# A block of small matmuls on a constant tile, run ahead of the first norm of a hybrid RWKV-7 / attention encoder

## The chip, the cores and the metric

The kernel runs on one core of one Trainium2 chip. The time is that of the device, in microseconds (us), for one execution of the whole program. The median of three runs before the change is 4313.76 us (4312.27 to 4315.98). The core has five engines that this text names by the profile's short names: PE (TensorE, matmuls; PEld is its weight loads, which overlap with the matmuls), DVE (VectorE), ACT (ScalarE), POOL (GpSimd) and SP (SyncE, which here issues DMAs). Each works through its own instructions in order and waits on semaphores for the others.

## The reference

Two requests, 256 and 1024 tokens of 1024 channels, go through the same two layers. Layer 0 mixes tokens with a bidirectional RWKV-7 recurrence, layer 1 with neighbourhood attention, and each is followed by a squared-ReLU MLP. Everything is float32. The part around the change is the very start: the norm of layer 0, the token-shift mixes that read the normalised `h`, and the first projections.

```python
def _rms_norm(x, g):
    xf = x.astype(jnp.float32)
    y = xf * lax.rsqrt(jnp.mean(jnp.square(xf), axis=-1, keepdims=True) + RMS_EPS)
    return y.astype(x.dtype) * g

def _rwkv7_mixer(h, ...):
    zero = jnp.zeros_like(h[:, :1])
    xx = 0.5 * (jnp.concatenate([zero, h[:, :-1]], axis=1) + jnp.concatenate([h[:, 1:], zero], axis=1)) - h
    r, k, v = jnp.einsum('sbtc,scd->sbtd', h[None] + xx[None] * mix[:3, None, None, :], w_rkv)
    xw = h + xx * mix[3]
    xa = h + xx * mix[4]
    xg = h + xx * mix[5]
...
def _trunk(x, p):
    for layer in range(DEPTH):
        h = _rms_norm(x, p['norm_mix_g'][layer])
        ...
```

## The kernel before

Both requests lie side by side as 1280 token columns, channels on the partitions in eight tiles of 128 (`KT`). The columns are cut into three segments, 256, 512 and 512 (`SEGS`). A dense product is made of three matmuls on reduced-precision halves of its operands (`mm3`, lines 95 to 99): each operand is split into a high and a low part, a weight by ACT's copy (line 91) and POOL's subtraction (line 92), an activation by ACT (line 166) and DVE (line 167). Plain float32 operands are used elsewhere, in the norm among others.

`l0_proj` (from line 102) is the first stage. SP loads `h` by segments, and the first three blocks of `w_k` between them (`early`). `norm(s)` (line 140) squares the eight channel tiles of a segment on ACT (line 147, two buffers), sums them over the channels with a float32 matmul against a tile of ones (line 148), so that each output row holds the sum, takes the inverse root on DVE and ACT (lines 152 and 1192 to 1196) and scales `h` in place on DVE (line 155). `mix` (line 157) then makes one of the six mixes of one channel tile: ACT (161), POOL (163), DVE (164), and the split (166, 167). `project` runs the dense products of `w_k` (lines 97 to 99 again) with the mixes of later segments and two LoRA products (`lora_first`, mixes by `mix2`, lines 173 to 184, split 271 and 272) put between them. The norms of the three segments stand at the head of the queue `mixq` of mixes.

In this stage no order is written out by hand: a scheduler places the instructions of each engine, by the order in the program and by its own idea of when each is ready. From `prep_open` on, at about 317 us, PE, DVE, ACT and POOL follow an order that is written by hand through due times (`at`), within `tc.manual_schedule`. The recurrence, the output layer, attention and the second layer come after that.

PSUM, in which matmuls write, is given out in pools. The stage opens `pnA` (one tile) and `pdA` (four tiles `ps`, two of `lps`), each tile 128 x 512 float32. SBUF pools with `side="right"` (`hp`, `wkA`, `wpA`) lie at the other end of SBUF from the rest (`mixp`).

Rows of other lines that the text uses as prices: lines 292 (sums of squares of k, 512 columns), 607 (LoRA second products, weights on 64 partitions, the two directions on the two partition halves in turn), 903 and 921 (32 x 32 tiles), 953 and 1023 (128 x 128 float32), 1613 (two columns), 1845 and 1876 (attention's output, 64 weight columns, the two heads on the two column halves in turn).

Of the kernel before, what the change touches and what calls it, by code (L numbers as in the profile page):

```python
# [5 lines left out]
F32 = mybir.dt.float32  # L6
# [4 lines left out]
PSUM = bass.MemoryType.PSUM  # L11
DRAM = bass.MemoryType.DRAM

P = 128
# [34 lines left out]
class Trunk:  # L49
# [49 lines left out]
        mm(ps, sl, mh, start=False, stop=last)  # L99


    def l0_proj(self):
        nc, tc, a = self.nc, self.tc, self.a
        k_d = self.dram("k_d", [8, P, T])
# [7 lines left out]
        pos = [1, 258, 770]  # L112
        W = 1283

        mixctx = ExitStack()
        mixp = mixctx.enter_context(tc.tile_pool(name="mixp", bufs=1))
        hctx = ExitStack()
# [224 lines left out]
        w = [self.wsplit(wp, a["w_r"][m], 1024, nc.gpsimd, hb=3, rb=1) for m in range(2)]  # L342
# [1618 lines left out]
```

## Time and profile before

| what | value |
|---|---|
| median of three runs | 4313.76 us |
| the profiled execution | 4314.01 us |
| its span, first to last instruction | 4312.1 us |
| mean granted TensorE clock | 0.958 |
| first load of `h` issued | 1.64 us |
| first matmul of the norm | 5.95 us |
| DVE's first step of the first norm | 12.95 us |
| hand-ordered part begins | about 317 us |

Times in the views are microseconds from the first instruction. A timeline row has the start, the length, the engine, the line of the kernel, the operation, the tiles (output <- inputs), rows * columns of the weight, the shape of the moving tile, its type as the profile shows it, and a count of merged records; in brackets stands the idle time before it and what ended it. A row of one line's instructions gives the count and the shortest, the median and the longest duration in ns. A stage row has the length, and for each engine the busy time and the number of instructions. Matmuls are pipelined, so a record's length includes the time until its result has left the array; how fast records follow each other is read from their starts.

### The profile page before, as it was taken

What the parts mean: (1) busy time and instruction counts of PE and PEld (TensorE: products, weight loads), DVE (VectorE), ACT (ScalarE), POOL (GpSimd) and SP (SyncE); (2) the same over time, 40 slices, a digit from 0 to 9 for tenths busy, and PEclk for the clock granted to TensorE, in tenths of its full rate; (3) what the DMA queues carried; (4) which work ended last, traced back from release to release, by engine and by line L of the source; (5) the groups of instructions that cost most, each with busy time, mean ns of one, the idle gap of its engine ahead of it and who ended that gap; (6) DMA issues with size and microseconds to landing.
All of it is one profiled execution on the core that took longest, in us unless ns stands there. A gap on an engine that the chain in (4) does not pass through costs nothing.

```text
span 4312.1 us, 69598 instructions
## 1 busy us (share of the span) xinstructions
PE 3991.1 (93%) x25060; PEld 3342.6 (78%) x25060; DVE 2660.7 (62%) x5390; ACT 1813.1 (42%) x4803; POOL 1426.1 (33%) x1498
## 2 busy tenths in 40 slices
PE   7888878888998879999999998999998999999999
PEld 4665668777777758888888888877676888888888
DVE  7889963577787654755555555166665655555555
ACT  6766641677777753111111123355554311111111
POOL 5440001234444443422222234144444432222222
PEclk9997879899999989999999999999998999999999
DMA  3335565566666434111111104333335211111111
GB/s 120 81 107 198 196 201 144 141 157 155 153 151 153 108 97 133 38 39 36 40 35 40 40 31 152 117 72 77 78 70 161 65 40 40 40 35 39 35 40 59
DMA packets 484537, 400.25 MB, mean 93 GB/s; under 512 B 289216, under 2 KB 392864, under 8 KB 484192
## 3 DMA queue, kind: packets, MB, share of 16 engines
q1 hardware_dynamic: 447968, 328.56, 28.1%
q10 hardware_dynamic: 34416, 61.35, 3.9%
q0 software_dynamic: 1808, 5.90, 0.4%
q8 instruction: 197, 3.23, 0.3%
q14 instruction: 148, 1.21, 0.1%
HBM read 285.66 MB, written 121.24 MB: 94 GB/s over the span
## 4 chain that ended last, share of the span: by engine, by line
PE 69%; DVE 14%; ACT 6%; DMA 5%; issue 4%; POOL 2%; SPq 1%; ACTq 0%; DVEq 0%; POOLq 0%
PE ps L97 17%; PE ps L99 16%; PE ps L98 16%; PE w L1060 2%; PE us L1032 2%; PE kps L953 1%; PE aps L812 1%; PE vps L503 1%; PE vps L505 1%; PE vps L504 1%; PE op L1876 1%; PE us L1046 1%; PE w L1012 1%; DVE S L1054 1%; ACT u L1041 1%
## 5 line engine op out<-in xcount | busy, mean ns | idle before, releaser
L1433 DVE TENSOR_TENSOR x<-ps,x 128x256 f32<-128x256 f32 x1488 | 814.1, 595 | 628.3 <-PE ps L99 628.0
L97 PE MATMUL ps<-ah,whi 128*128 128x512 f32 (+1 forms) x2304 | 843.1, 366 | 5.0 <-ACT whi L91 4.2
L99 PE MATMUL ps<-ah,wlo 128*128 128x512 f32 (+1 forms) x2304 | 824.0, 358 | 2.1 <-POOL wlo L92 2.0
L98 PE MATMUL ps<-al,whi 128*128 128x512 f32 (+1 forms) x2304 | 823.5, 357 | 2.6 <-POOL al L1323 2.6
L92 POOL TENSOR_TENSOR wlo<-raw,whi 128x1024 fp32r<-128x1024 f32 (+1 forms) x178 | 390.5, 2194 | 851.9 <-ACT whi L91 807.8
L97 PE MATMUL ps<-hh,whi 128*128 128x512 f32 (+1 forms) x1536 | 546.9, 356 | 13.8 <-DVE x L1433 13.8
L99 PE MATMUL ps<-hh,wlo 128*128 128x512 f32 (+1 forms) x1536 | 545.9, 355 | 0.0
L98 PE MATMUL ps<-hl,whi 128*128 128x512 f32 (+1 forms) x1536 | 545.2, 355 | 0.0
L97 PEld LDWEIGHTS ps<-ah,whi 128*128 128x128 f32 x2304 | 438.8, 190 | 80.2 <-issue 13.1
L91 ACT CAST whi<-raw 128x1024 fp32r<-128x1024 f32 (+1 forms) x206 | 200.7, 975 | 696.5 <-PE ps L98 630.6
L99 PEld LDWEIGHTS ps<-ah,wlo 128*128 128x128 f32 x2304 | 437.8, 190 | 67.8 <-POOL wlo L92 2.9
L98 PEld LDWEIGHTS ps<-al,whi 128*128 128x128 f32 x2304 | 438.5, 190 | 63.0 <-POOL al L1323 2.9
L1412 POOL TENSOR_TENSOR rl<-rl 128x512 f32<-128x512 f32 (+1 forms) x192 | 174.3, 908 | 500.6 <-PE ps L99 458.3
L97 PEld LDWEIGHTS ps<-hh,whi 128*128 128x128 f32 x1536 | 291.4, 190 | 57.4 <-DVE x L1433 16.8
L1411 ACT ACTIVATE rl<-ps 128x512 f32<-128x512 f32 (+1 forms) x192 | 100.8, 525 | 546.4 <-PE ps L99 546.4
L98 PEld LDWEIGHTS ps<-hl,whi 128*128 128x128 f32 x1536 | 291.4, 190 | 41.0
L99 PEld LDWEIGHTS ps<-hh,wlo 128*128 128x128 f32 x1536 | 291.4, 190 | 41.1
L1414 ACT CAST hh<-rl 128x512 fp32r<-128x512 f32 (+1 forms) x192 | 105.5, 549 | 321.0 <-POOL rl L1412 320.9
L1054 DVE SCALAR_TENSOR_TENSOR S<-us,dall,sd 64x64 f32<-64x64 f32 x512 | 145.0, 283 | 126.4 <-PE us L1046 115.7
L1415 DVE TENSOR_TENSOR hl<-rl,hh 128x512 fp32r<-128x512 f32 (+1 forms) x192 | 119.4, 622 | 151.6 <-ACT hh L1414 151.1
L1016 POOL TENSOR_TENSOR sd<-S,dall 128x128 f32<-128x128 f32 x256 | 122.5, 480 | 258.2 <-DVE S L1054 174.8
L1060 PE MATMUL w<-u,zb 128*128 128x128 f32 x640 | 158.2, 330 | 47.0 <-ACT u L1041 44.8
(310 smaller groups left out, 8222.4 us busy)
## 6 DMA issues: line engine op xcount, KB each, us to landing
raw<-in_w_down_dram SPq DMA_DIRECT2D x64, 512.0 KB, 3.5
raw<-in_w_up_dram SPq DMA_DIRECT2D x64, 512.0 KB, 3.4
ar<-ar_d SPq DMA_DIRECT2D x80, 256.0 KB, 3.4
bk<-bk_d SPq DMA_DIRECT2D x80, 256.0 KB, 3.5
ar_d<-ar ACTq DMA_DIRECT2D x32, 512.0 KB, 2.7
bk_d<-bk ACTq DMA_DIRECT2D x32, 512.0 KB
bs<-tab SPq DMA_DIRECT2D x128, 96.0 KB, 3.9
v_d<-vt ACTq DMA_DIRECT2D x80, 128.0 KB, 4.0
```

The lines of the kernel that those rows point to most:

```text
L91: nc.scalar.copy(hi[:, cs], raw)
L92: lo_eng.tensor_tensor(out=lo[:, cs], in0=raw, in1=hi[:, cs].bitcast(F32), op=ALU.subtract)
L97: mm(ps, sh, mh, start=first, stop=False)
L98: mm(ps, sh, ml, start=False, stop=False)
L99: mm(ps, sl, mh, start=False, stop=last)
L1016: nc.gpsimd.tensor_tensor(out=R["sd"], in0=st["S"], in1=self.dall[:, m, d, ch:ch + 1].to_broadcast([P, P]), op=ALU.mult)
L1054: nc.vector.scalar_tensor_tensor(out=S2[es, es], in0=sn[es, es], scalar=D, in1=R["sd"][es, es], op0=ALU.mult, op1=ALU.add)
L1060: nc.tensor.matmul(w, J["zb"][d, g][:, c, :], R["u2"], start=False, stop=True, skip_group_check=True)
L1412: nc.gpsimd.tensor_tensor(out=r[:, :n], in0=r[:, :n], in1=r[:, :n], op=ALU.mult)
L1414: nc.scalar.copy(hh[:, :n], r[:, :n])
L1415: nc.vector.tensor_tensor(out=hl[:, :n], in0=r[:, :n], in1=hh[:, :n].bitcast(F32), op=ALU.subtract)
L1433: nc.vector.tensor_tensor(out=xv, in0=ps[:, :n], in1=xv, op=ALU.add)
```

## The change

A method `small_products` is added, and `l0_proj` calls it ahead of all its pools. It fills one SBUF tile with ones (DVE), opens eight PSUM tiles, and issues twelve loops of float32 matmuls, 286 in all, with that tile as both operands. PE keeps to the order written. `full` uses the whole 128 x 128 array. `quad(r, c, ...)` takes 64 partitions (row half `r`) and by default 64 weight columns that go to output partitions of column half `c`; with `64, 128` it uses a row half and all 128 columns. The last loop uses all rows and a column half. Both pools are closed before the stage opens its own. Nothing reads the eight tiles.

```diff
+    def small_products(self):
+
+        nc, tc = self.nc, self.tc
+        mm = nc.tensor.matmul
+        with tc.tile_pool(name="prw", bufs=1) as sp, tc.tile_pool(name="prp", bufs=1, space=PSUM) as pp:
+            x = sp.tile([P, 512], F32, name="prx")
+            nc.vector.memset(x, 1.0)
+            b = [pp.tile([P, 512], F32, name=f"pr{i}") for i in range(8)]
+            w = x[:, 0:P]
+
+            def quad(r, c, n, i, k=64, m=64):
+                rs = slice(k * r, k * r + k)
+                mm(b[i][m * c:m * c + m, :n], w[rs, :m], x[rs, :n], start=True, stop=True)
+
+            def full(n, i):
+                mm(b[i][:, :n], w, x[:, :n], start=True, stop=True)
+            with tc.manual_schedule(engines={mybir.EngineType.PE}):
+                for i in range(14):
+                    full(512, i % 8)
+                for i in range(24):
+                    full(128, i % 8)
+                for i in range(24):
+                    full(64, i % 8)
+                for i in range(24):
+                    quad(i % 2, i % 2, 64, i % 2)
+                for i in range(24):
+                    quad(0, i % 2, 64, i % 2 * 2)
+                for i in range(32):
+                    quad(i % 2, i // 2 % 2, 64, i % 4)
+                for i in range(24):
+                    quad(i % 2, i // 2 % 2, 128, i % 4)
+                for i in range(24):
+                    quad(i % 2, 0, 128, i % 2, 64, 128)
+                for i in range(24):
+                    quad(i % 2, 0, 64, i % 2, 64, 128)
+                for i in range(8):
+                    full(128, i % 2)
+                    quad(0, 0, 64, 2)
+                    quad(1, 1, 64, 3)
+                for i in range(8):
+                    quad(i % 2, 0, 128, 4 + i % 2, 64, 128)
+                    quad(0, 0, 64, 2)
+                    quad(1, 1, 64, 3)
+                for i in range(24):
+                    mm(b[i % 8][64 * (i % 2):64 * (i % 2) + 64, :64], w[:, :64], x[:, :64], start=True, stop=True)
...
     def l0_proj(self):
...
         pos = [1, 258, 770]
         W = 1283
 
+        self.small_products()
         mixctx = ExitStack()
```

## The prediction

> **What bounds the kernel now.** I read the page's first part, then the timeline and the chain of waits of the first 110 us, then tables by stage, and last the rows of small matmuls anywhere in the span that can price the new ones. A difference under 0.2% (8.6 us) can't be told from no change here; the three runs of before span 3.7 us.
>
> ```profile
> span 4312.1 us, 69598 instructions
> PE 3991.1 (93%) x25060; PEld 3342.6 (78%) x25060; DVE 2660.7 (62%) x5390; ACT 1813.1 (42%) x4803; POOL 1426.1 (33%) x1498
> ```
>
> Over the span TensorE (PE) is the busiest. The change sits at the very start, though, and there another engine decides. PE's timeline of that start (start, length, engine, line, tiles, shape, count):
>
> ```profile
> 5.95 4.65 PE L148 MATMUL ps<-sq,ones 128*128 128x256 f32 x10 [5.95 <-ACT sq L147]
> 11.01 6.87 PE L148 MATMUL ps<-sq,ones 128*128 128x256 f32 x16 [0.41 <-ACT sq L147]
> 19.25 1.12 PE L148 MATMUL ps<-sq,ones 128*128 128x512 f32 x2 [1.37 <-ACT sq L147]
> 28.16 5.46 PE L148 MATMUL ps<-sq,ones 128*128 128x512 f32 x8 [7.79 <-ACT sq L147]
> ```
>
> PE does nothing before 5.95 us, while the first inputs are loaded, and has long holes later. Stage by stage (length; busy PE, PEld, DVE, ACT, POOL; granted clock; DMA share; GB/s):
>
> ```profile
> 13.00:33.00 20.00, 10.78 (x19) 3.75 (x20) 16.77 (x29) 15.04 (x30) 9.70 (x11) 0.74 0.56 201
> 33.00:57.00 24.00, 16.92 (x92) 11.34 (x90) 20.44 (x25) 12.46 (x23) 10.88 (x7) 0.97 0.26 83
> 57.00:85.00 28.00, 22.23 (x74) 15.16 (x75) 28.00 (x28) 18.30 (x30) 20.43 (x15) 0.85 0.02 9
> 85.00:110.00 25.00, 24.63 (x100) 15.78 (x99) 14.24 (x22) 15.35 (x30) 12.13 (x12) 1.00 0.40 138
> 110.00:150.00 40.00, 36.92 (x232) 30.70 (x231) 35.82 (x60) 31.87 (x68) 16.21 (x19) 1.00 0.29 55
> 150.00:200.00 50.00, 42.33 (x237) 32.20 (x236) 45.30 (x74) 36.73 (x81) 25.22 (x27) 0.97 0.29 88
> 200.00:250.00 50.00, 44.75 (x273) 33.70 (x272) 47.60 (x92) 38.30 (x98) 23.55 (x31) 1.00 0.35 118
> 250.00:300.00 50.00, 44.74 (x199) 32.84 (x200) 48.30 (x64) 36.07 (x70) 29.02 (x25) 0.93 0.12 41
> ```
>
> From 13 us on VectorE (DVE) is full: 28.00 of 28.00 from 57 to 85 us, and 256.47 of the 287 us of all eight rows. What it works on hangs on the first norm, since every mix reads the normalised h. DVE's first piece of that is this row, and everything behind it starts later by as much as this row does:
>
> ```profile
> 12.95 0.42 DVE L152 TENSOR_SCALAR nx<-ps 128x256 f32<-128x256 f32 x1 [9.23 <-PE ps L148]
> ```
>
> **The change, part by part.** It adds one DVE memset and 286 float32 matmuls on PE. They write eight PSUM tiles of 128x512 float32. The norm's PSUM pools are opened after the block's pool has been closed and take its space over, so I have PE run the whole block before the norm's first matmul. Inside it PE waits for the memset alone, and nothing reads the results.
>
> *What one record costs.* L148 (below) shows 16 records of 256 columns for the eight matmuls of the first norm, and the page has as many weight loads (PEld) as matmul records: a float32 matmul is two records, each with its own weight load, though L148's weight (ones) never changes. So the constant tile saves no loads. Prices are pitches: (length of a burst − length of one) / (count − 1).
>
> ```profile
> L148 PE MATMUL ps<-sq,ones x48: 379/594/1222, 5.9 to 41.3; 128*128 128x512 f32 x32, 128*128 128x256 f32 x16
> 921.25 0.61 PE L953 MATMUL kps<-ar,bdk 128*128 128x128 f32 x4
> L953 PE MATMUL kps<-ar,bdk x640: 275/275/582, 744.9 to 1531.4; 128*128 128x128 f32 x160
> 96.10 1.03 PE L292 MATMUL nps<-ksq,cst 128*16 128x512 f32 x2
> L292 PE MATMUL nps<-ksq,cst x6: 592/597/603, 87.3 to 96.5; 128*16 128x512 f32 x6
> 2762.01 0.95 PE L1613 MATMUL nst<-cst,sq 128*128 128x2 f32 x8
> L1613 PE MATMUL nst<-cst,sq x320: 165/251/352, 2756.0 to 3238.9; 128*128 128x2 f32 x160
> ```
>
> - 128 wide, whole array: (0.61 − 0.275)/3 = 0.112 us a record, 0.223 a matmul.
> - 512 wide: 1.03 − 0.60 = 0.43 a record, 0.86 a matmul.
> - 2 wide: (0.95 − 0.25)/7 = 0.100. A record of 2 columns costs nearly what one of 128 does, so a full weight load sets a floor of about 0.10; 64 wide lies between, 0.106.
>
> ```profile
> 2874.21 0.40 PE L99 MATMUL ps<-ah,wlo 128*128 128x512 f32 x1
> 2874.54 0.45 PE L1845 MATMUL op<-s,vs 128*64 128x64 f32 x8
> 2874.92 0.50 PE L97 MATMUL ps<-ah,whi 128*128 128x512 f32 x1
> 2875.26 0.39 PE L98 MATMUL ps<-al,whi 128*128 128x512 f32 x1
> 2875.49 0.40 PE L99 MATMUL ps<-ah,wlo 128*128 128x512 f32 x1
> L1845 PE MATMUL op<-s,vs x128: 222/222/369, 2805.4 to 3273.7; 128*64 128x64 f32 x128
> 2812.45 0.88 PE L1876 MATMUL op<-s,vs 128*64 128x128 f32 x12
> L1876 PE MATMUL op<-s,vs x732: 272/273/476, 2812.4 to 3295.0; 128*64 128x128 f32 x183
> 390.04 1.02 PE L607 MATMUL l<-ta,wa 64*128 64x512 f32 x4
> 1017.08 0.40 PE L903 MATMUL yps<-qx,zb 32*32 32x32 f32 x13
> L903 PE MATMUL yps<-qx,zb x1280: 191/191/258, 752.2 to 1537.3; 32*32 32x32 f32 x183
> ```
>
> - 64 wide, two column halves in turn: (0.45 − 0.222)/7 = 0.033.
> - 128 wide in halves: with a single one at 0.273, (0.88 − 0.273)/11 = 0.055, half of the whole array's 0.112: two halves run at once.
> - Two row halves: four 512-wide records in 1.02 us, where the whole array would need 3 × 0.43 + 0.60 = 1.89: at once as well. Row and column in turn: (0.40 − 0.191)/12 = 0.017 for 32-wide tiles.
> - Going from whole to tiled and back: L1845 starts 0.33 after L99 where 0.23 is the pitch (2875.26 to 2875.49), +0.10; L97 starts 0.15 after the last tiled record (2874.54 + 0.45 − 0.22 = 2874.77) where a pair's pitch is 0.066, +0.08; the next record comes after 0.34, +0.11. About 0.30 a round trip.
>
> *The sum.* The twelve loops in their order, in us, with low and high in brackets. Low is the smallest pitch or four tiles at once; high is tiles strictly in turn, twice the paired pitch.
> 1. 14 × 512: 14 × 0.86 = 12.0, plus a slow start. The norm's first ten records of 256 columns take 4.65 us, about 0.45 each once the last one's tail is taken off, twice the 0.215 that half of 0.43 would be; the second run, from 11.01 on, has full speed in it (L148's shortest record takes 0.379). That is some 5 us at half speed, a loss of 2.5 (1.7 to 3.4). 14.5 (13.7; 15.4).
> 2. 24 × 128: 5.4 (5.4; 5.4). 3. 24 × 64: 48 × 0.106 = 5.1 (4.8; 5.4).
> 4. and 5. 24 quads each, 64 wide: 48 × 0.033 = 1.6 each (1.6; 3.1). 6. 32 quads over four tiles: 64 × 0.033 = 2.1 (1.1; 4.2).
> 7. 24 quads, 128 wide: 48 × 0.055 = 2.6 (1.3; 5.3).
> 8. and 9. 24 row halves with a 128-wide weight: 48 × 0.056 = 2.7 each (2.7; 5.4).
> 10. 8 × (whole + two quads): 0.223 + 4 × 0.033 + 0.30 = 0.65, 5.2 (2.9 with no switch cost; 6.0).
> 11. The same with a row half for the whole: 5.2 (2.8; 6.0). No row shows a row half against a quarter; I take the price of the only switch shown.
> 12. 24 column halves: 1.6 (1.6; 3.1). The other switches between loops: 0.7 (0; 1).
>
> Together 51 us (42; 69).
>
> [...]
>
> *Where it lies.* PE can begin once the memset is done. The nearest row is GpSimd's memset of a quarter of the size, and it also shows when engines are let go:
>
> ```profile
> 0.74 0.20 POOL L134 MEMSET ones<- 128x128 f32 x1 [0.29 <-POOLq L1949]
> ```
>
> 0.74 + 0.2 to 0.8 + a handoff: 1.4 (1.0; 1.8). The block ends at 1.4 + 51 = 52.4. The norm's squares wait in ScalarE's two buffers; the rest of the norm is PE and ScalarE in turn, eight steps at a warm 0.45 (two 256-wide records 0.43) and a handoff, 3.8 us, so nx starts at 56.2 instead of 12.95: **+43.2**. What hides part: before, this stretch was partly DMA time, and that is over by then; it is in the 3.8 against 7.0 (5.95 to 12.95) already.
>
> More comes back behind it. Weight casts (ScalarE) and their low parts (POOL) of three w_k blocks and the first LoRA weight don't need the norm, and can run in the block. Before, they got in DVE's way:
>
> ```profile
> 21.54 4.06 DVE L167 TENSOR_TENSOR ml<-mu,mh 128x256 fp32r<-128x256 f32 x3
> 27.06 1.50 DVE L167 TENSOR_TENSOR ml<-mu,mh 128x256 fp32r<-128x256 f32 x3
> 34.99 2.18 DVE L1194 TENSOR_TENSOR nt<-nr 128x512 f32<-128x512 f32 x1 [2.48 <-ACT nr L1193]
> 46.01 0.82 DVE L1194 TENSOR_TENSOR nt<-nr 128x512 f32<-128x512 f32 x1 [1.36 <-ACT nr L1193]
> 21.29 2.52 POOL L92 TENSOR_TENSOR wlo<-raw,whi 128x1024 fp32r<-128x1024 f32 x1
> 34.24 2.38 POOL L256 TENSOR_TENSOR lw<-lraw,lw 128x1024 fp32r<-128x1024 f32 x1
> ```
>
> Beside a POOL low part the same DVE work takes 2.6 and 1.4 longer, and the wait before L1194 is 1.1 longer: 5 us that can go. At most 10: these 4.0 and nearly all of DVE's idle from 13 to 57 us (3.2 + 3.6, less what the norm's own steps need). At least 0. I take 5: **+38**.
>
> Nothing downstream has room to take it back: the stage is full on DVE (rows above) until the hand-ordered part, which moves as a whole. The profiled execution took 4314.01 us, 1.9 around its span; 4314.0 + 38 = 4352. It lies 0.25 above the median, so the forecast for the median is the same.
>
> **The rivals.**
> *Tiles in turn.* Loops 4 to 12 gain nothing from halves, or the queue can't feed them so fast: block 69, +18 on the forecast, 4370. For it: the bursts above have 4 to 13 records, while here some 350 follow each other, and a burst may live from what was queued. Against it: every tiled row runs in pairs. [...]
> *Shorter and better covered.* Block 42 and 10 regained: 43.2 − 8.8 − 10 = +24, 4338. For it: four tiles at once need only the spacing of L903's records; ScalarE and POOL have 50 us to run ahead.
> *Not slower.* The first stage's order comes from a scheduler, not by hand, and shifts with the norm. If the new order closed DVE's holes up to the hand-ordered part, 287 − 256.5 = 30.5 us, and the POOL collisions, 4.0, it would leave 43.2 − 34.5 = +8.7, at the edge of no change: 4322. It decides only if nearly every hole closes, and they are waits in a chain of dependent steps (L1194 waits for ScalarE).
> *The block isn't there.* Nobody reads its results; dropped at compile time, it leaves a memset under the wait for DMA: 4314. Nothing in the trace shows unread work, so neither for nor against.
>
> **How the numbers follow.** Forecast 0.62 (4343 to 4361), tiles in turn 0.15, shorter 0.17, not slower 0.03, not there 0.03. The range reaches to both rivals on the slow side: 4338 to 4370; left out are the last two and the outer parts of the other rivals, under 0.2. Slower by over 0.2% 0.94, within 0.05, faster 0.01 (the not-slower case overshooting).
>
> **What would show it.** Right: about 572 new PE records ending near 52 us, nx at 56, DVE busy without holes from there, tiled loops at 0.03 to 0.06 a record, the rest of the timeline as before but later by some 38 us. Wrong: nx much before 45 or after 70; loop 11 without switch costs; wlo still beside the mixes (then +43); or a shift that shrinks between 85 and 300 us.

## The result, and the profile after

The changed kernel takes 4352.89 us in the median of three runs (4352.88 to 4353.92), against 4313.76 before: a ratio of 1.0091 with a 95% interval of 1.0068 to 1.0114. That is 39 us slower, where 38 were forecast. Its profiled execution took 4352.88 us with a span of 4351.1, so the time around the span is 1.8 us, as before. The mean granted clock is 0.959 (before 0.958).

The page's first part, after:

```profile
span 4351.1 us, 70740 instructions
PE 4038.9 (93%) x25632; PEld 3379.3 (78%) x25632; DVE 2656.5 (61%) x5391; ACT 1813.5 (42%) x4803; POOL 1426.1 (33%) x1498
```

There are 572 more matmul records, 286 times two, and as many more weight loads; one more DVE instruction is the memset. PE is busy 47.8 us longer. Nothing else has more to do. Lines of the old code stand 47 further down from here on (the norm's matmul L148 is L195).

PE's timeline of the start, after (of loop 10 only the first round and the start of the second are shown, and a row can merge several loops):

```profile
1.46 24.48 PE L117 MATMUL pr<-prx 128*128 128x512 f32 x124 [1.46 <-DVE prx L108]
25.87 10.76 PE L114 MATMUL pr<-prx 64*64 64x64 f32 x304
36.56 0.49 PE L117 MATMUL pr<-prx 128*128 128x128 f32 x2
36.98 0.33 PE L114 MATMUL pr<-prx 64*64 64x64 f32 x4
37.24 0.49 PE L117 MATMUL pr<-prx 128*128 128x128 f32 x2
...
41.74 6.98 PE L114 MATMUL pr<-prx 64*64 64x64 f32 x52
48.65 2.83 PE L146 MATMUL pr<-prx 128*64 128x64 f32 x48
51.63 5.07 PE L195 MATMUL ps<-sq,ones 128*128 128x256 f32 x16 [0.16 <-PE pr L146]
```

The block runs without a gap from 1.46 to 51.63 us, 50.2 us, and the norm's first matmul starts at its end, where it started at 5.95 before. DVE's first step of the norm, and the last `mu` of the first 24 mixes (the second row; before it was at 84.84, in the third):

```profile
56.75 0.42 DVE L199 TENSOR_SCALAR nx<-ps 128x256 f32<-128x256 f32 x1 [53.02 <-PE ps L195]
...
124.83 1.10 DVE L211 SCALAR_TENSOR_TENSOR mu<-ms,hm,mu 128x512 f32<-128x512 f32 x1
```

```profile
84.84 1.10 DVE L164 SCALAR_TENSOR_TENSOR mu<-ms,hm,mu 128x512 f32<-128x512 f32 x1
```

So `nx` is 43.8 us late, and 68 us further on DVE is 40.0 us late: 3.8 us have come back. The start of the hand-ordered part in the two kernels (before, then after):

```profile
303.94 0.17 DVE L549 TENSOR_SCALAR hw<-vec 128x32 f32<-128x32 f32 x1
```

```profile
346.35 0.17 DVE L596 TENSOR_SCALAR hw<-vec 128x32 f32<-128x32 f32 x1
```

It is 42.4 us late there, and at the end of the span 39.0. Matching DVE's instructions one by one, the delay goes up and down in between, from some 34 us (34.0 at 1531 us of before) to some 45 (44.6 at 3141 us). DVE works in the same order there as before, and PE nearly so. The first fall, from 42.4 to 37.4 within 130 us of that start, goes with a higher granted clock. Two stages of 100 us from that start on (length; busy PE, PEld, DVE, ACT, POOL; granted clock; DMA share; GB/s), first before, then after:

```profile
304.00:404.00 100.00, 81.70 (x277) 51.49 (x276) 75.33 (x141) 61.37 (x129) 0.00 (x0) 0.69 0.58 203
```

```profile
346.30:446.30 100.00, 80.20 (x286) 50.31 (x285) 79.44 (x147) 65.07 (x136) 0.00 (x0) 0.73 0.60 210
```

After, the clock is higher and PE gets nine more records done in the same 100 us.

The block itself, with the clock, by stages of the same form:

```profile
14.00:42.00 28.00, 28.00 (x451) 25.47 (x451) 0.00 (x0) 4.18 (x4) 9.43 (x5) 1.00 0.52 183
42.00:45.00 3.00, 3.00 (x30) 2.25 (x26) 0.00 (x0) 0.00 (x0) 0.00 (x0) 1.00 0.21 81
45.00:49.00 4.00, 4.00 (x30) 2.79 (x30) 0.00 (x0) 0.00 (x0) 0.00 (x0) 0.57 0.00 0
49.00:52.00 3.00, 2.84 (x49) 2.68 (x46) 0.00 (x0) 0.00 (x0) 0.00 (x0) 0.50 0.00 0
52.00:57.00 5.00, 4.49 (x17) 2.37 (x16) 0.25 (x1) 3.18 (x8) 0.00 (x0) 0.96 0.00 0
```

From 45.54 to 52.37 us the granted clock was halved, though PE had been busy without a gap for 44 us. Loop 11 runs there, and loop 12. The first row also shows what ACT and POOL did meanwhile: four casts, and as many low parts with the end of an earlier one. Their own timelines have `whi` at 10.59, 17.78 and 26.45, `wlo` at 11.71, 18.90 and 27.57, and `lw` on POOL at 29.90 and 37.61, all before the first mix.

The twelve loops, each from the start of its first record to that of the next loop's first, against the forecast:

| loop | forecast us (low; high) | measured us |
|---|---|---|
| 1: 14 x 512 | 14.5 (13.7; 15.4) | 13.66 |
| 2: 24 x 128 | 5.4 | 5.36 |
| 3: 24 x 64 | 5.1 (4.8; 5.4) | 5.40 |
| 4: quads, both halves in turn | 1.6 (1.6; 3.1) | 1.40 |
| 5: quads, column halves in turn | 1.6 (1.6; 3.1) | 1.35 |
| 6: four quads in turn, 64 wide | 2.1 (1.1; 4.2) | 0.97 |
| 7: four quads in turn, 128 wide | 2.6 (1.3; 5.3) | 1.46 |
| 8: row halves, 128 wide | 2.7 (2.7; 5.4) | 2.78 |
| 9: row halves, 64 wide | 2.7 (2.7; 5.4) | 2.72 |
| 10: whole and two quads | 5.2 (2.9; 6.0) | 5.44 |
| 11: row half and two quads | 5.2 (2.8; 6.0) | 6.65 |
| 12: column halves | 1.6 (1.6; 3.1) | 2.99 |
| switches between loops | 0.7 (0; 1) | within the above |
| all | 51 (42; 69) | 50.2 |

### The profile page after: what moved, and what is told of

Read it like the earlier page. It is cut to its first block, busy times and chain, and to the rows that moved or that the text cites. A ratio compares the mean times of both kernels' runs of the same rounds, so it can differ in the third digit from the quotient of the medians.

```text
span 4351.1 us, 70740 instructions
## 1 busy us (share of the span) xinstructions
PE 4038.9 (93%) x25632; PEld 3379.3 (78%) x25632; DVE 2656.5 (61%) x5391; ACT 1813.5 (42%) x4803; POOL 1426.1 (33%) x1498
## 4 chain that ended last, share of the span: by engine, by line
PE 70%; DVE 13%; ACT 6%; issue 3%; DMA 3%; POOL 2%; SPq 1%; ACTq 0%; DVEq 0%; POOLq 0%
PE ps L97 17%; PE ps L99 16%; PE ps L98 16%; PE w L1107 2%; PE us L1079 2%; PE kps L1000 2%; PE vps L550 1%; PE vps L552 1%; PE vps L551 1%; PE aps L859 1%; PE w L1059 1%; ACT u L1088 1%; PE us L1093 1%; ACT u L1074 1%; DVE S L1101 1%
## 5 line engine op out<-in xcount | busy, mean ns | idle before, releaser
L99 PEld LDWEIGHTS ps<-ah,wlo 128*128 128x128 f32 x2304 | 437.9, 190 | 67.8 <-POOL wlo L92 2.7
L98 PEld LDWEIGHTS ps<-hl,whi 128*128 128x128 f32 x1536 | 291.7, 190 | 41.1
```

The source lines that it names most:

```text
L98: mm(ps, sh, ml, start=False, stop=False)
```

## The experiments

Theory A throughout is the prediction's: the time grows by what `nx` is delayed, less a small fixed sum that the casts give back, and by nothing else. The rivals stand in each expectation. The runs of the kernel before that ran beside the experiments had medians of 4311.95 to 4316.16 us, each with a spread of 16 to 23 us from its fastest to its slowest, so ratios are to the runs on the same chip, and a gain or loss given as "about" is worked out from the ratio. The traces carry what the times can't tell: `nx`, and the last `mu` of the first 24 mixes, called "mix 24" below. Between them lie 71.9 us before and 68.1 after.

**The block cut short, doubled, or only its memset.** Three kernels have loops 1 to 3 alone, the whole block twice, and no matmul at all:

```diff
             with tc.manual_schedule(engines={mybir.EngineType.PE}):
                 for i in range(14):
                     full(512, i % 8)
                 for i in range(24):
                     full(128, i % 8)
                 for i in range(24):
                     full(64, i % 8)
-                for i in range(24):
-                    quad(i % 2, i % 2, 64, i % 2)
...
```

> Loops 4 to 12 are left out; the block then ends near 25.9 us. Theory A (what counts is how late the first norm ends; that is passed on whole, less some 4 us that the weight casts give back): nx at about 30.7 us, 17.8 later than in the kernel before, time +14 (+11 to +18), about 4328. Theory B (the rest of the stage takes back a fixed share: 39.1 us lost for 50.2 of block, 0.78): 0.78 x 24.4 = +19, 4333. Theory C (added PE work costs wherever it stands): +24.

Measured: 4334.6 us, ratio 1.0044 (1.0027 to 1.0061), about +19. The block ran from 1.46 to 27.50 (loop 1 took 15.07 here), and `nx` started at 32.73, +19.8. That is just beyond theory A's +11 to +18 and equal to theory B's +19; with an interval of +12 to +26 the time alone does not part them. The trace shows where theory A's sum was off: loop 1 took longer, and mix 24 came 71.3 us after `nx`, so 0.6 us came back instead of 3.8. Timelines of DVE and of POOL in this run:

```profile
35.62 6.42 DVE L180 SCALAR_TENSOR_TENSOR h<-h,vec,nr 128x256 f32<-128x256 f32 x8
```

```profile
37.68 2.53 POOL L281 TENSOR_TENSOR lw<-lraw,lw 128x1024 fp32r<-128x1024 f32 x1
```

The last low part runs at the same time as in the full block (37.61, where ACT's cast of it waited for the load `lraw` until 36.49), but here DVE is already scaling `h` beside it, and that takes 6.42 us where it takes 4.33 in the kernel after: 2.1 of the 3.2 us that are missing. Most of the rest is a wait of 1.17 us for the second norm's sum, which the kernel after doesn't have. So the give-back isn't a fixed sum: a block of 26 us, which ends before the last cast, brings hardly any.

```diff
+                for rep in range(2):
+                    for i in range(14):
+                        full(512, i % 8)
...
```

> The twelve loops run twice. Theory A: the block ends near 100 us, nx at about 105, 92 later than before, time +88 (+84 to +93), about 4402. Theory B: 0.78 x 99 = +77, 4391.

Measured: 4408.39 us, ratio 1.0213 (1.0197 to 1.0228), about +92. The second copy ended at 102.70, `nx` came at 107.46, +94.5, and mix 24 67.8 us after it: 4.1 us came back. This is theory A's +84 to +93; a give-back that grows with the block, at +77, is out.

```diff
-            with tc.manual_schedule(engines={mybir.EngineType.PE}):
-                for i in range(14):
-                    full(512, i % 8)
...
+            pass
```

> All matmuls are left out; memset and pools stay. Every theory in which the matmuls cost the time: no change, 4310 to 4318. If it is the memset, the pools or the placement of code that costs: up to +39.

Measured: 4315.73 us, ratio 0.9999 (0.9988 to 1.0011). The memset, the eight PSUM tiles and the two pools cost nothing that can be told from no change; `nx` to mix 24 is 71.9 us, as before. In the traced execution `nx` is nevertheless 2.05 us late, at 15.00, and the hand-ordered part 4.1. So a few microseconds there differ from trace to trace without added matmuls.

**Does the shape of the matmuls matter, or the time they take?** Here 220 plain 128-wide products on the whole array stand in place of the twelve loops, so as to last about as long with no tiles and no switches:

```diff
             with tc.manual_schedule(engines={mybir.EngineType.PE}):
-                for i in range(14):
-                    full(512, i % 8)
...
+                for i in range(220):
+                    full(128, i % 8)
```

> 220 whole-array matmuls, 128 wide, in place of the twelve loops: 220 x 0.223 = 49.1 us warm, some 2 more for the slow start. Theory A: the content does not matter; nx near 57.5, +44.5, time +40 (+36 to +45), about 4354. If tiles, or the half clock that loops 11 and 12 of the change ran at, weigh on what follows: clearly less, +30 to +35.

Measured: 4361.48 us, ratio 1.0104 (1.0089 to 1.0119), about +45. The block ran from 1.46 to 52.90, `nx` came at 57.66, +44.7, and 68.1 us lie from there to mix 24. The downstream behaves as in the kernel after, to 0.1 us, so the tiled products leave nothing behind them that shows there. The time lies at the upper edge of the +36 to +45 expected, with an interval of +38 to +51. The clock was whole where it was halved after, so here 50 us of busy PE did not bring that about (stage of this run):

```profile
45.00:52.00 7.00, 7.00 (x65) 7.00 (x64) 0.00 (x0) 0.00 (x0) 0.00 (x0) 1.00 0.00 0
```

**Where does the halved clock come from?** In the kernel after it began in loop 11 and covered loop 12. One run puts loop 12 ahead of loops 10 and 11; another, with about 270 us of matmuls, runs one pattern after the other, each for 15 us or more, with whole 512-wide products between them.

```diff
+                for i in range(24):
+                    mm(b[i % 8][64 * (i % 2):64 * (i % 2) + 64, :64], w[:, :64], x[:, :64], start=True, stop=True)
                 for i in range(8):
                     full(128, i % 2)
...
-                for i in range(24):
-                    mm(b[i % 8][64 * (i % 2):64 * (i % 2) + 64, :64], w[:, :64], x[:, :64], start=True, stop=True)
```

> Loop 12 stands ahead of loops 10 and 11. Theory K (loops 10 and 11 keep the array too little occupied, and the clock is halved for that): loop 12 takes 1.4 us instead of 2.99, the clock still falls in loop 11 or after it, the norm then starts 1.5 earlier or so. Rival (tiles on column halves, or the time since the start, halve the clock): loop 12 at 2.8 again, or the clock falls at 45 us whatever runs there.

Measured, one run: 4362.73 us. Its stages, by loop (12, then 10, then 11 in two parts, then the norm):

```profile
37.14:38.69 1.55, 1.55 (x50) 1.48 (x49) 0.00 (x0) 0.34 (x1) 1.14 (x1) 1.00 0.00 0
38.69:44.13 5.44, 5.44 (x52) 3.93 (x49) 0.00 (x0) 0.00 (x0) 1.21 (x1) 1.00 0.32 99
44.13:46.71 2.58, 2.58 (x28) 1.90 (x24) 0.00 (x0) 0.00 (x0) 0.00 (x0) 1.00 0.00 0
46.71:51.64 4.93, 4.77 (x29) 3.24 (x27) 0.00 (x0) 0.00 (x0) 0.00 (x0) 0.50 0.00 0
51.64:56.95 5.31, 5.31 (x13) 3.30 (x13) 0.00 (x0) 2.08 (x5) 0.00 (x0) 0.50 0.00 0
```

Loop 12 takes 1.55 us at the whole clock, the forecast's 1.6; its 2.99 in the kernel after is about twice that, at the halved clock. Loop 10 leaves the clock alone. The fall comes 2.6 us into loop 11, and the low clock then lies over the norm: the block ends at 51.64, as after, and not 1.5 earlier as expected, and `nx` comes at 58.35, 1.6 later. The hand-ordered part begins at 346.4 in both, so the other 10 us by which this one run is longer than the kernel after arise behind it and don't belong to the order of the loops.

```diff
+                for i in range(24):
+                    full(128, i % 2)
+                    quad(0, 0, 64, 2)
+                    quad(1, 1, 64, 3)
+                for i in range(20):
+                    full(512, i % 8)
+                for i in range(24):
+                    quad(i % 2, 0, 128, 4 + i % 2, 64, 128)
+                    quad(0, 0, 64, 2)
+                    quad(1, 1, 64, 3)
+                for i in range(20):
+                    full(512, i % 8)
...
```

> In place of the twelve loops: seven streams of some 8 to 16 us each, with 20 matmuls 512 wide ahead of each to bring the clock up: whole array 128 wide; loop 10's pattern; loop 11's pattern; two quarters in turn (loop 4); four quarters (loop 6); two row halves (loop 8); one row half alone. Theory K: the clock is halved in the patterns of loops 10 and 11 and perhaps in the row half alone, and stays whole in the others. Rival: it is halved in all tiled streams, or in none but by chance. Time: about +230 (8 x 17 of 512 wide and some 95 of streams).

Measured, one run: 4569.57 us, +258 where +230 was expected. Stages of it: loop 10's pattern; whole products; loop 11's pattern in two parts; whole products in two parts; 64-wide quads:

```profile
54.00:70.00 16.00, 16.00 (x144) 11.53 (x143) 0.00 (x0) 0.00 (x0) 0.00 (x0) 1.00 0.01 1
70.00:87.40 17.40, 17.40 (x44) 7.52 (x40) 0.00 (x0) 0.00 (x0) 0.00 (x0) 1.00 0.00 0
87.40:91.40 4.00, 4.00 (x37) 2.93 (x36) 0.00 (x0) 0.00 (x0) 0.00 (x0) 1.00 0.00 0
91.40:111.75 20.35, 20.35 (x112) 14.13 (x109) 0.00 (x0) 0.00 (x0) 0.00 (x0) 0.50 0.00 1
111.75:115.35 3.60, 3.60 (x7) 1.53 (x6) 0.00 (x0) 0.00 (x0) 0.00 (x0) 0.50 0.00 0
115.35:126.00 10.65, 10.65 (x26) 4.75 (x25) 0.00 (x0) 0.00 (x0) 0.00 (x0) 1.00 0.00 0
130.00:148.00 18.00, 18.00 (x546) 16.63 (x545) 0.00 (x0) 0.00 (x0) 0.00 (x0) 1.00 0.01 4
```

In these rows the clock is halved in loop 11's pattern alone. It falls 4.0 us after the pattern begins, stays down as long as it lasts, and comes back 3.6 us after whole products have taken over. Loop 10's switching from whole to quads (16.00 us), quads in pairs (15.96 us) and four quads in turn (14.20 us from 164.00 on) ran at 1.00, and so did row halves in turn in the kernel after (5.50 us, 31.00 to 36.50). So theory K, as it was posed, is half right: the clock falls in a switching pattern, but not in the one from the whole array. Loop 11's pattern ran in five places in all (after, both copies of the doubled block, the reordered block, the probe). The fall came 3.5 us after its start in the kernel after (42.00 to 45.54), 2.6 in the reordered block and 4.0 in the probe; in both copies of the doubled block loop 12, behind it, has a row of 2.83 us, as it has after, where it has 1.62 at the whole clock in the reordered block.

The probe also has 800 records of four quads in turn, a longer burst than any in the block. PE's timeline of it:

```profile
164.15 3.25 PE L114 MATMUL pr<-prx 64*64 64x64 f32 x207
168.37 2.09 PE L114 MATMUL pr<-prx 64*64 64x64 f32 x128 [0.97 <-issue]
172.10 2.09 PE L114 MATMUL pr<-prx 64*64 64x64 f32 x128 [1.64 <-issue]
175.55 2.09 PE L114 MATMUL pr<-prx 64*64 64x64 f32 x128 [1.36 <-issue]
```

The records run at 0.016 each, as in loop 6, but after some 200 of them PE begins to stand idle without a wait that the profile shows (`issue`): 128 records every 3.45 us (172.10 to 175.55), 0.027 each. What it waits for there is not shown. Quads in pairs, 540 records in 15.89 us or 0.029 each, come just slower than that and run without a gap.

**Is it the work or its place?** The same 220 products, now beside the norm and the first mixes, on the norm's tile of ones and with the lowest priority:

```diff
-        self.small_products()
+        prp = hctx.enter_context(tc.tile_pool(name="prp", bufs=1, space=PSUM))
+        prb = prp.tile([P, 512], F32, name="pr0")
...
+        for i in range(220):
+            nc.tensor.matmul(prb[:, :P], ones, ones, start=True, stop=True)
         while extra:
             extra.pop(0)()
```

> The same 220 matmuls on the tile of ones, into one PSUM tile of a pool that is open beside the norm's, and written behind the stage's projections, so that the scheduler uses them where PE has nothing else ready. Theory A (the delay of the first norm is the cost): the norm is late by a microsecond at most, nx at 12 to 15 us, time -3 to +8, 4311 to 4322. Theory C (49 us more PE work cost 40 us wherever they stand): +35 to +45.

Measured: 4350.73 us, ratio 1.0083 (1.0066 to 1.01), about +36 (+39 by the medians): theory A's expectation failed, and the number is theory C's. The trace shows where. Only 134 of the 440 records found room in PE's holes before 66 us, at a delay of some 3 us. Most of the rest ran together, 286 records in this row of PE's timeline, before the stage's pools could close:

```profile
289.52 32.84 PE L360 MATMUL pr<-ones 128*128 128x128 f32 x286
```

DVE's delay was 3.6 us up to there and 35.6 behind it. The run didn't tell work from place, since most of the work had only moved to another place on the path. So the number that did fit, 67 products, was run by itself, beside the norm and ahead of it:

```diff
-        for i in range(220):
+        for i in range(67):
             nc.tensor.matmul(prb[:, :P], ones, ones, start=True, stop=True)
```

> Two kernels with the same added work, 67 plain 128-wide float32 products (134 records, about 15.0 us at 0.112), told apart only by their place. This one has them beside the norm and the first mixes, with the lowest priority, on the tile of ones; they are the number that found room before 66 us in e6_128_wide_beside, where they cost some 3 us. Theory A (the change costs what it delays the norm by; matmul work put into TensorE's holes is nearly free): nx at 11 to 13 instead of 12.95, VectorE 0 to 5 us later between 60 and 300 us, no lump of added products behind 100 us, and the time +0 to +5 us, not told apart from before. Theory C (the matmul work itself is the cost, wherever it stands): +10 to +15.

```diff
-                for i in range(14):
-                    full(512, i % 8)
...
+                for i in range(67):
+                    full(128, i % 8)
```

> The same 67 products ahead of the norm. Block 1.46 to about 18 (134 x 0.112 and 1.6 for the slow start), nx at 18.1 + 5.1 = 23.2, +10.2. Theory A: the casts of the first weights are only begun by then, so 0 to 1 us comes back as in e1_loops_1_to_3: +9 to +12, and more than e9_67_beside by 6 us or more. Rival (a 5-us start is free in any case, as in e8_short_warm_up, and the scheduler takes up more of a short delay than of a long one): +0 to +6.

Measured: beside the norm 4318.18 us, ratio 1.001 (1.0 to 1.0021); ahead of it 4325.79 us, ratio 1.0029 (1.0019 to 1.0039). PE's timelines of the two, beside and then ahead:

```profile
1.00 4.42 PE L360 MATMUL pr<-ones 128*128 128x128 f32 x22 [1.00 <-POOL ones L154]
...
20.17 4.41 PE L360 MATMUL pr<-ones 128*128 128x128 f32 x38
```

```profile
1.46 17.42 PE L117 MATMUL pr<-prx 128*128 128x128 f32 x134 [1.46 <-DVE prx L108]
19.03 4.72 PE L169 MATMUL ps<-sq,ones 128*128 128x256 f32 x16
```

Ahead, the block ends at 19.03 and `nx` comes at 23.78, +10.8; the time grew by 12.5 (0.29% of 4315.0; 10.8 by the medians), and mix 24 comes 12.8 later, so nothing came back and 2.0 more were lost. The interval, +8 to +17, leaves out the rival's +0 to +6. Beside, `nx` came at 10.95 and the hand-ordered part began 3.7 us later than before; the time grew by 4.3 (0 to 9). The same records cost about 8 us less in the holes (7.6 by the medians). Whether they cost 3 to 4 there or nothing is not shown: the second and the third `nx` come 0.5 and 3.5 us late in this trace, but the hand-ordered part was 4.1 late with the memset alone. The kernels beside the norm also have a PSUM tile of their own, so no run tells whether the norm waits for the block by PE's order or for the PSUM space that the block holds.

**Is the slow start worth anything?** Two 512-wide products and one 256-wide, over before the first square is ready:

```diff
-                for i in range(14):
-                    full(512, i % 8)
...
+                for i in range(2):
+                    full(512, i)
+                full(256, 2)
```

> Only two matmuls 512 wide and one 256 wide, at half clock about 4.3 us, from 1.46 to about 5.8, so over before the norm could start. Theory A: nothing is late, and the norm's first matmuls may run at full clock earlier: 0 to -2 us, 4311 to 4316, no difference to be told. If every added PE microsecond costs: +4.

Measured: 4315.63 us, ratio 1.0003 (0.999 to 1.0016). The norm's sixteen records then run at the whole clock (4.72 us from 6.22 on) and `nx` comes at 10.98, 2.0 us earlier; but mix 24 comes at 84.28 against 84.84, so 1.4 of the 2.0 are lost again at once, and the time shows no difference (+1, with an interval of -4 to +7, which doesn't leave out +4). A warm-up is no gain here, and no other run pointed to a version faster than the kernel before.

## Why the prediction was right

The mechanism was the one forecast: the norm waits for the block, DVE's mixes wait for the norm, and a few microseconds come back. That the sum came out within 1 us is partly luck, since several terms were off by 1 to 3 us, some up and some down.

*The norm waits for the whole block.* Right: L195 starts at 51.63, when L146 is done, and its idle time ends on PE's own `pr`. That the length of the block is what counts, and not its kind, is shown by the kernels of the experiments: +19.8, +44.7 and +94.5 at `nx` gave about +19, +45 and +92 in time.

*The block's length, 51 us.* Measured 50.2, but two errors of nearly 3 us meet in it. Loops 4 to 7 took 5.2 us where the forecast had 7.9. In loops 6 and 7 the low bound was right: 64 records in 0.97 us are 0.015 each, half of the 0.029 of a pair in loop 4, so four quarters do run at once; I had taken a pair's pitch since no row showed four 64-wide tiles. In the probe's long burst, with its idle time, it is 0.027. Loop 1 took 0.8 less than the 14.5 forecast, since the clock came up 3.1 us after the block's start and not after 5. Against that, loops 11 and 12 took 9.6 where 6.8 stood, by the halved clock. The forecast had no term for it, though a stage of before shows a busy PE at the halved clock (row halves of L607 and weights of 16 rows, L680):

```profile
318.20:328.44 10.24, 9.88 (x22) 3.69 (x20) 5.39 (x11) 7.74 (x19) 0.00 (x0) 0.50 0.72 246
```

Loop 11's first rounds, at the whole clock, follow each other at 0.68 us, and so do loop 10's: 5.4 for eight, where 5.2 had been taken for both.

*The switch in loop 11.* The price of a switch, taken from whole against halves since no row showed this pair, was right in size: a row half against quarters costs the same 0.68 a round as whole against quarters, not the 0.35 of the low case (2.8 for eight rounds). Why the switch costs that, no run shows.

*The norm behind the block, 3.8 us.* It took 5.1 (51.63 to 56.75). ACT's timeline, after:

```profile
52.70 0.85 ACT L194 ACTIVATE sq<-h 128x256 f32<-128x256 f32 x2 [15.17 <-PE ps L195]
53.91 0.85 ACT L194 ACTIVATE sq<-h 128x256 f32<-128x256 f32 x2 [0.36 <-PE ps L195]
55.11 0.85 ACT L194 ACTIVATE sq<-h 128x256 f32<-128x256 f32 x2 [0.36 <-PE ps L195]
```

With two buffers ACT and PE take turns, at 1.2 us for two channel tiles, where I had 0.45 for each. Behind the plain block, at the whole clock, the norm took 4.76 (52.90 to 57.66), so 1.0 of the 1.3 is the turn-taking and 0.3 the halved clock, up to 52.37. The +43.2 was therefore +43.8.

*What comes back, 5 us.* Measured 3.8 at mix 24, and 3.5 to 4.1 in the other blocks of 50 us and more. By DVE's rows it is made of three parts. From the first norm's `nx` to the second's lie 18.87 us before (12.95 to 31.82) and 14.54 after (56.75 to 71.29): 4.3 back, where 2.6 had been forecast. The mixes and splits that no longer meet a low part are 2.5 of it, near the forecast; another 1.57 is DVE's wait for the second norm's sum, which is gone, and the last of the splits now stands behind `nx`. DVE's row before, then its rows after:

```profile
31.82 0.69 DVE L152 TENSOR_SCALAR nx<-ps 128x512 f32<-128x512 f32 x1 [1.57 <-PE ps L148]
```

```profile
71.29 0.68 DVE L199 TENSOR_SCALAR nx<-ps 128x512 f32<-128x512 f32 x1
...
74.62 0.69 DVE L1241 TENSOR_TENSOR nt<-nr 128x512 f32<-128x512 f32 x1 [2.31 <-ACT nr L1240]
...
86.12 0.69 DVE L1241 TENSOR_TENSOR nt<-nr 128x512 f32<-128x512 f32 x1 [3.34 <-ACT nr L1240]
```

From the second `nx` to that norm's scaling lie 6.84 and 5.50: 1.3 back, where 2.5 had been forecast. L1194 (now L1241) is no longer slowed by a low part (2.18 before, 0.69 in the row at 74.62), but the wait ahead of it, of which 1.1 had been counted on, is nearly the same, 2.48 and 2.31. From the third norm's `nx` to its scaling lie 4.36 and 6.20: 1.8 lost. That loss was not foreseen. The row at 86.12 is the third norm's: DVE waits there for ACT, and ACT sits at a copy of the projection's result that isn't ready (ACT's timeline, after):

```profile
83.99 0.37 ACT L331 COPY kt<-ps 128x256 f32<-128x256 f32 x1 [1.69 <-PE ps L99]
84.40 0.51 ACT L334 ACTIVATE ksq<-kt,vec 128x256 f32<-128x256 f32 x1
84.81 0.61 ACT L1239 ACTIVATE nt<-nx 128x512 f32<-128x512 f32 x1
```

`nx` was done at 82.78 and its next step on ACT began at 84.81, behind the copy; before, the copy began at 43.38 and was over when `nx` came at 43.96. So the collisions were rightly named as the cause of most of the term, and it was 1 us too large.

*The rest moves as a whole.* Right in the main: between 85 and 300 us the delay doesn't fall below the 40.0 of mix 24. But it grows, to 41.1 (90 to 170 us of before) and 42.5 (most of 180 to 300), and this was not followed. At the end 39.0 are left. The first fall in that last part goes with the clock, as the two stages of 100 us show; that the clock is the whole of it is not shown, since the delay goes on moving between some 34 and 45 us. That these steps add up to 3.4 is luck.

*The rivals.* Tiles in turn is out: loops 4 to 9 took 10.7 us, less than the forecast's 13.3, and not twice that. Its argument that a long burst slows down fits the probe, where PE stands idle after 207 records, whatever the cause; but the 0.027 a record that is left there lies below a pair's pitch, 0.029, and the one loop that is faster has 64 records. The block is there. The shorter block with 10 us back is out on both terms, though its price for four tiles at once was the right one. Not slower is out: only 1.4 of the 43.8 us are gone where the hand-ordered part begins, and one of DVE's holes grew.

## What to carry to other kernels

Work put ahead of the first thing that a full engine waits for costs nearly all of its length, however idle its own engine is (39 of 50.2 us here: 4.5 lay before the norm could have begun, the norm behind it took 5.1 instead of 7.0, and some 4 came back), so read its price from its last record and not from the busy share; 67 products in the holes cost about a third of what they cost ahead, with an interval that reaches down to nothing, and more than the holes hold went onto the path later. Price tiled matmuls by how many tiles of the array work at once (0.029 us a record here for 64-wide quads in pairs, 0.015 for four in turn), and a change of tile shape by the round, 0.68 us here whether it comes from the whole array or from a row half. After an early delay look at each engine's queue for work that has slipped ahead of the step that others wait for.

## What the runs showed of the hardware

In a pattern of a 128-wide row half and two quarters in turn the granted clock was halved, 2.6 us (reordered block), 3.5 (after) and 4.0 (probe) after its start, although PE had no gap up to there. With the whole array in place of the row half it stayed at 1.00 for 16.00 us of the probe, and so it did for quads in pairs (15.96 us), four quads in turn (14.20 us) and, in the kernel after, row halves in turn (5.50 us). An account that fits, an estimate of mine from the records' pitches, is how much of the array is at work over time: by the whole-array pitch (0.112 us for 128 columns), loop 10 has two such records and four records of a quarter of the array and about half that length in 0.68 us, some 0.4 of the array's time, and loop 11 has half of the former, some 0.25. Quads in pairs hold half of the array at most, and kept the clock whole. No run varied the share by itself, so the cause is argued and not shown.

The traces of before and after fit it, though. In both, the granted clock changes only at marks 3.41 us apart, whose place differs from run to run: after, it rises at 4.58, falls at 45.54, 12 steps on, and rises at 52.37, two more; before, it rises at 11.01 and falls at 21.25, three steps on. The 3.5 us before the fall in loop 11 end at such a mark. Reckoned from mark to mark in the same way, at 0.43 us for a record of 512 columns (0.23 in the dense products), there are 1769 stretches in the two traces with PE busy for at least 95% of the time and the clock whole. It fell after one alone: that of loop 11 from 42.13 on, with a share of 0.24. None of the others is below 0.37. With PE as busy and the clock halved, as in the stage of before at 318.20, it rose after 1 of 19 stretches with a share under 0.35, and after 75 of 76 with one over 0.45.

PE stood idle at `issue` in the probe's four quads in turn after 207 records, and then did 128 every 3.45 us.

The first records ran slowly until the clock came up, at 4.58 us after the change: the 512-wide ones begin 0.85 to 1.01 us apart up to 4.18, and 0.43 apart from 4.81 on. The 124 records of loops 1 to 3 took 24.48 us there. Written alike, they took 25.07 in the reordered block, 25.89 in loops 1 to 3 alone, and 25.66 and 23.92 in the two copies of the doubled block, the second of which begins at 52.74.
